# Leftover expert blocks: the down projection of one block stands behind the up projection of the next

## The chip, the cores and the metric

The kernel runs on one core of one Trainium2 chip. TensorE (PE) multiplies matrices, VectorE (DVE) and ScalarE (ACT) work on tiles, GpSimd (POOL) issues the transfers whose rows are picked by an index (gathers and scatters), SyncE (SP) issues most of the plain ones. Each engine carries out its own instructions in the order in which the program lists them, and they meet through semaphores. The metric is the device time of one execution in microseconds.

## The reference

One layer of a decoder on 512 tokens of width 1024: a mixer (three causal branches, gated, projected back and added to the stream) and then a mixture of experts. Only the second half touches the change:

```
h     = adaLN-modulated rmsnorm(x)                       # 512 x 1024
ids, weight = the top 8 of 64 experts for each token     # group-limited, sigmoid
for expert e, for each token t that chose it:
    y = ((silu(h[t] @ w1[e]) * (h[t] @ w3[e])) @ w2[e])  # 1024 -> 256 -> 1024
    out[t] += 2.5 * weight * y
out += shared expert(h)
result = rmsnorm(x + gate * out, final_norm)
```

## The kernel before, in words

The mixer fills the first part of the span. Then a router sorts the tokens by expert, and its result lies in a table in memory: for each run of up to 128 tokens of one expert, the tokens' numbers and their weights, which are loaded on chip as `idxw`. The runs are worked off in two stages. The stage of pairs takes most of them (`pair_of_runs`). What is left, runs that found no place in a pair, is the **leftover stage**: 96 blocks are written out, block i inside `tc.If(n_left > i)`, each If nested in the one before (L1369 to L1371), so that the program jumps out of the nest after the last block there is. With this input nine blocks run, 0 to 8. All of it stands under `tc.manual_schedule()`: what an engine carries out is in the order in which the code is written.

One block takes 128 rows of tokens through one expert, in fp32 by splitting a number into a high and a low part:

- `load_up` (SP): w1 and w3 of block i+2 into `ra[i % 2]`, two transfers of 1 MB each. `load_down` (SP, L1012): w2 into `rad`, 1 MB.
- **Up projection** (PE, L1153 to L1155): 24 matmuls of 128x512 (eight steps of k; high by high, high by low, low by high), out of `mT` (the block's rows, transposed and split; `h2T` in the code) and `wh`, `wl` (the split weights) into `ph`. The weights of block i+1 are split meanwhile (`split_a`: `wh` by ACT L49, `wl` by DVE L50).
- `act_a`: silu (ACT L1162), then the product with the other half and the token's weight (DVE L1163) into `hw`.
- `x_a` twice: eight transposes (PE L1146) of `xg`, the rows gathered for block i+1, and their split into `mT` (ACT L49, DVE L50).
- `turn_b`: two transposes of `hw` (PE L1278) and a copy to `hb` (ACT L1280).
- `gather_a` (POOL): a copy of the token numbers for block i+2 (L1118) and their gather into `xg` (L1120).
- `down_b`: four matmuls, `hb` by w2 (PE L1288, each fp32 matmul is two records in the trace), and the product with the layer's gate into `y` (DVE L1289, two halves).
- `add_a` (POOL L1191): the scatter that adds `y` to the rows of `acc2` in memory.

POOL's gathers and scatters go through one software queue (q0 in the profile), the plain loads through another (q1). Behind the nest `acc2` is read back (`rc<-acc`, L1378, SP and ACT), the sum is normed and written out.

Of the kernel before, what the change touches and what calls it, by code (L numbers as in the profile page):

```python
# [20 lines left out]
P = 128  # L21
# [13 lines left out]
def trunk(ctx, tc, x, c, ada_w, ada_b, norm1, norm2, w_in, conv_a_w, conv_a_b, ln_a_g, ln_a_b,  # L35
# [796 lines left out]
    def rt(shape, name, dt=F32, bufs=1, tag=None):  # L832
        return hp.tile([P] + shape, dt, name=name, bufs=2 if tag in ("x1", "h2", "tm", "hf2") else bufs, tag=tag or name)
# [198 lines left out]
    V.scalar_tensor_tensor(cls[:, 1], svf, 64.5, cls[:, 2], op0=OP.is_lt, op1=OP.mult)  # L1032
    for j in range(2):
        V.tensor_tensor_scan(cum[:, j], ones, cls[:, j], (2.0, 0.0)[j], op0=OP.mult, op1=OP.add)
    nn_, mi = rt([2], "nn_"), rt([3], "mi", I32)
    V.scalar_tensor_tensor(mi[:, 0:1], cum[:, 0, P - 1:], 31.0, cum[:, 1, P - 1:], op0=OP.min, op1=OP.min)
    V.tensor_scalar(mi[:, 1:2], mi[:, 0:1], 1, None, op0=OP.logical_shift_right)
    V.tensor_scalar(nn_[:, 0:1], mi[:, 1:2], 2.0, None, op0=OP.mult)
# [8 lines left out]
    V.tensor_tensor(L[:, 0], cls[:, 2], lf[:, 0], op=OP.subtract)  # L1047
    V.tensor_tensor_scan(cl_, ones[:, 0:1].to_broadcast([P, 2 * P]), L.rearrange("p a e -> p (a e)"), nn_[:, 1:2], op0=OP.mult, op1=OP.add)
    V.tensor_copy(mi[:, 2:3], cl_[:, 2 * P - 1:])
    it, jk2, th = rt([5], "it"), rt([2 * P], "jk2", tag="tm"), rt([1], "th")  # L1050
    V.scalar_tensor_tensor(jk2[:, :P], cum[:, 0], iop, ones, op0=OP.is_le, op1=OP.mult, accum_out=it[:, 0:1])
    V.scalar_tensor_tensor(jk2[:, :P], cum[:, 1], iop, ones, op0=OP.is_le, op1=OP.mult, accum_out=it[:, 1:2])
# [25 lines left out]
    for a, src in enumerate((v_, c_)):  # L1078
# [1 line left out]
        for j in range(3):  # L1080
            T.matmul(ips[:, j], src[:, j:j + 1], ident, start=True, stop=True)
        V.tensor_copy(iv[:, a], ips)
    V.tensor_copy(items[:, 6, 0:2], mi[0:1, 1:3])
    hst.close()
    rawst.close()


    n_four = nc.values_load(items[0:1, 6, 0:1], min_val=0, max_val=15)
    n_left = nc.values_load(items[0:1, 6, 1:2], min_val=0, max_val=NL)
    ep = est.enter_context(tc.tile_pool(name="ep", bufs=1))  # L1090
    psx = est.enter_context(tc.tile_pool(name="psx", bufs=1, space=PSUM))
    xg = [ep.tile([P, D], F32, name=f"xg{b}") for b in range(2)]
# [22 lines left out]
    def gather_a(row, j, n=2):  # L1115
        s = j % 2
        cl = G.value_load(items[0:1, row + 1, j:j + 1], min_val=0, max_val=4 * E - 1)
        G.tensor_copy(ia[s], idxw[:, ds(cl, 2)])  # L1118
        for b in range(n):
            G.indirect_dma_start(out=xg[b], out_offset=None, in_=h2d, in_offset=IOA(ap=ia[s][:, b, 0:1], axis=0),  # L1120
                                 bounds_check=S - 1, oob_is_err=False)

    def gather_c(row, j):
        s = j % 2
# [6 lines left out]
    def slots(src, shape, name):  # L1131
        t = ep.tile([P] + shape, I32, name=name, bufs=2)
        V.tensor_copy(t, src)
        return t

    def split_a(j, u, up=None):
        if u < 4:
            src = (up or ra[j % 2]).rearrange("p (z k f) -> p k z f", z=2, k=KT)[:, 2 * u:2 * u + 2]
            split(*(w[u].rearrange("p (k z f) -> p k z f", k=2, z=2) for w in (wh, wl)), src)
        else:  # L1140
            split(wh[u], wl[u], rad[j % 2][:, (u - 4) * 1024:(u - 3) * 1024])

    def x_a(b, g):
        pt = psx.tile([P, 4, P], F32, name="pt", bufs=2)
        for k in range(4):
            T.transpose(pt[:, k], xg[b][:, (g * 4 + k) * P:(g * 4 + k + 1) * P], ident)  # L1146
        split(h2T[0][b][:, g * 4:g * 4 + 4], h2T[1][b][:, g * 4:g * 4 + 4], pt)
# [42 lines left out]
    def add_a(y, at, beside=None, to=acc):  # L1190
        st = G.indirect_dma_start(out=to, out_offset=IOA(ap=at, axis=0), in_=y, in_offset=None,  # L1191
                                  compute_op=OP.add, bounds_check=S - 1, oob_is_err=False)
        g = beside or f"run {st.ins.name}"
        if beside:
            tc.declare_no_dep(st.ins, group=g, reason="the rows of a run are distinct")
        tc.add_to_no_dep_group(g, st.ins)
        return g
# [77 lines left out]
    def turn_b(hw):  # L1275
        p3 = pse.tile([P, 2, 2, P], F32, name="p3")
        for k in range(2):
            T.transpose(p3[:, 0, k], hw[:, k * P:(k + 1) * P], ident)  # L1278
        hb = ew.tile([P, 2, P], F32, name="hb", tag="hh")
        A.activation(hb, p3[:, 0], AF.Copy)  # L1280
        return hb

    def down_b(i, hb):
        y = ew.tile([P, D], F32, name="y", bufs=2)
        for h in range(2):
            py, q = pse.tile([P, 512], F32, name="py", bufs=2), slice(h * 512, h * 512 + 512)
            for k in range(2):
                T.matmul(py, hb[:, k], rad[i % 2][:, k * 1024 + h * 512:k * 1024 + h * 512 + 512], start=(k == 0), stop=(k == 1))  # L1288
            V.tensor_tensor(y[:, q], py, gm2[:, q], op=OP.mult)  # L1289
        return y  # L1290

    def block(i):
        if i:
            load_up(ra, GL, i + 2)
        up = rc[0] if i == 1 else None
        ph = ps_up((0,))
        for u in range(4):
            up_a(ph, u)
            if u < 3:
                split_a(i + 1, u, up)  # L1300
        hw = act_a(ph[0], ia[i % 2][:, 0, 1:2])
        sa = slots(ia[i % 2], [2, 2], "sa")
        split_a(i + 1, 3, up)
        x_a(0, 0)
        x_a(0, 1)
        hT = turn_b(hw)
        gather_a(GL, i + 2, 1)
        add_a(down_b(i, hT), sa[:, 0, 0:1], to=acc2)
        load_down(rad[i % 2], GL, i + 2)

    gs, tok = rad[1][:, :D], ew.tile([P, TT], I32, name="tok")
    nc.sync.dma_start(gs, modr[3:4].to_broadcast([P, D]))
# [25 lines left out]
    with tc.manual_schedule():  # L1338
        gather_a(GA, 0)
        copied = gather_c(GC, 0)  # L1340
        for t in range(2):
            run = add_a(ysh[t], tok[:, t:t + 1], run)
        load_up(rc, GC, 0, copied)
        load_down(rcd, GC, 0)
        for g in range(4):
            x_a(g // 2, g % 2)
        gather_a(GA, 1)
        nc.sync.dma_start(fn[0:1], final_norm[None, :])
        A.activation(gm2, gs, AF.Copy)
        for z in range(2):  # L1350
            zq = slice(z * CH, z * CH + CH)
            A.activation(gm2c[zq], gs[zq, z * 512:z * 512 + 512], AF.Copy)
        for t in range(2, TT):
            run = add_a(ysh[t], tok[:, t:t + 1], run)
        for u in range(6):
            split_a(0, u)
        load_down(rad[1], GA, 1)
        with ExitStack() as nest:
            for i in range(15):
                nest.enter_context(tc.If(n_four > i))  # L1360
                pair_of_runs(2 * i)
                pair_of_runs(2 * i + 1)

        nc.scalar.dma_start(rc[1].rearrange("p (t d) -> p t d", t=TT), acc.rearrange("(t p) d -> p t d", p=P))
        for h in range(2):
            py, q = pse.tile([P, 512], F32, name="py", bufs=2), slice(h * 512, h * 512 + 512)
            T.matmul(py, ones[0:1], fn[0:1, q], start=True, stop=True)
            A.activation(fn[:, q], py, AF.Copy)
        with ExitStack() as nest:  # L1369
            for i in range(NL):  # L1370
                nest.enter_context(tc.If(n_left > i))  # L1371
                block(i)


    fs = ew.tile([P, TT], F32, name="fs")
# [41 lines left out]
```

## Time and profile before

| what | us |
| --- | --- |
| median of three runs | 1458.77 (1456.04 to 1461.76) |
| the profiled execution, its time | 1467.86 |
| the profiled execution, its span | 1466.1 |
| leftover stage, first up matmul of block 0 to the read of `acc2` | 1328.65 to 1445.83 |
| one block of it | 11.84 |

The prediction is worked out inside the profiled execution and then set against the median. Starts in the rows below count from the start of its span.

### The profile page before, as it was taken

To read this page: it belongs to the slowest core of one execution; us is meant where nothing else is said; L and a number is where in the kernel's file an instruction comes from. 1 tells how busy PE (TensorE), PEld (TensorE's weight loads), DVE (VectorE), ACT (ScalarE), POOL (GpSimd) and SP (SyncE) were. 2 spreads that over 40 slices of the span, in tenths; PEclk is the share of its full clock that TensorE was granted. 3 is DMA by queue.
4 is the path that set the end of the run, shared out by engine and by line. 5 is a ranking of instruction groups with operands and counts; after the bars stand their busy time and mean duration, and the time that the engine had idled before them with its cause. 6 is when DMAs were issued, how large, how long until landed. Compare 5 with 4: busy or idle time off the path is not lost. (4 is left out here: it accounts for less than half of the span.)

```text
span 1466.1 us, 24089 instructions
## 1 busy us (share of the span) xinstructions
PE 1347.5 (92%) x8982; PEld 968.7 (66%) x8982; DVE 956.0 (65%) x1816; ACT 620.3 (42%) x1019; POOL 264.8 (18%) x255
## 2 busy tenths in 40 slices
PE   4999999999999979998998978999999999997881
PEld 3877777776766756664686635777677777774660
DVE  6865998987777777233455855666656566564664
ACT  4454334427568658220212213434434443443442
POOL 1000000000000000000000354243342524333332
PEclk8999999999999989999999989999999999999996
DMA  9321231232112117759826348999898989966985
GB/s 339 110 58 31 66 89 47 69 125 92 31 59 80 31 51 237 242 185 333 278 74 238 134 154 266 371 341 322 322 313 294 314 301 337 321 219 206 317 285 208
DMA packets 120634, 289.13 MB, mean 197 GB/s; under 512 B 14883, under 2 KB 68397, under 8 KB 109486
## 3 DMA queue, kind: packets, MB, share of 16 engines
q1 hardware_dynamic: 99266, 242.87, 46.2%
q0 software_dynamic: 17904, 36.01, 10.0%
q10 hardware_dynamic: 3324, 8.49, 1.6%
q8 instruction: 75, 1.23, 0.3%
q14 instruction: 65, 0.53, 0.1%
HBM read 260.24 MB, written 46.97 MB: 210 GB/s over the span
## 5 line engine op out<-in xcount | busy, mean ns | idle before, releaser
L53 PE MATMUL ps_in<-hT_hi,w_hi 128*128 128x512 f32 x496 | 203.9, 411 | 2.7 <-ACT hT_hi L49 2.7
L54 PE MATMUL ps_in<-hT_hi,w_lo 128*128 128x512 f32 x496 | 201.5, 406 | 0.3 <-DVE w_lo L50 0.2
L55 PE MATMUL ps_in<-hT_lo,w_hi 128*128 128x512 f32 x496 | 199.9, 406 | 0.0
L50 DVE TENSOR_TENSOR wl<-ra,wh 128x1024 fp32r<-128x1024 f32 x100 | 122.1, 1224 | 115.2 <-ACT wh L49 111.6
L49 ACT ACTIVATE wh<-ra 128x1024 fp32r<-128x1024 f32 x100 | 105.6, 1060 | 127.8 <-PE ph L1155 90.0
L1153 PE MATMUL ph<-wh,mT_hi 128*128 128x512 f32 x328 | 134.5, 410 | 2.3 <-ACT wh L49 2.3
L1154 PE MATMUL ph<-wl,mT_hi 128*128 128x512 f32 x328 | 129.6, 395 | 0.5 <-DVE wl L50 0.5
L1155 PE MATMUL ph<-wh,mT_lo 128*128 128x512 f32 x328 | 129.3, 394 | 0.0
L50 DVE TENSOR_TENSOR w_lo<-w_raw,w_hi 128x1024 fp32r<-128x1024 f32 x76 | 92.5, 1223 | 51.0 <-ACT w_hi L49 50.8
L53 PEld LDWEIGHTS ps_in<-hT_hi,w_hi 128*128 128x128 f32 x496 | 94.6, 191 | 34.3 <-issue 7.6
L1191 POOL DMA_INDIRECT acc<-y,sa x41 | 65.6, 1599 | 272.9 <-DVE hc L1227 238.0
L54 PEld LDWEIGHTS ps_in<-hT_hi,w_lo 128*128 128x128 f32 x496 | 94.4, 190 | 21.7 <-issue 1.7
L55 PEld LDWEIGHTS ps_in<-hT_lo,w_hi 128*128 128x128 f32 x496 | 94.3, 190 | 21.8 <-issue 2.7
L49 ACT ACTIVATE w_hi<-w_raw 128x1024 fp32r<-128x1024 f32 x76 | 79.3, 1052 | 38.8 <-PE ps_p L55 18.3
L594 DVE SCALAR_TENSOR_TENSOR u<-ut,par,u 128x512 f32<-128x512 f32 x120 | 84.2, 747 | 0.6
L70 POOL TENSOR_TENSOR h<-h,mhalf 128x4 f32<-128x4 f32 x8 | 10.5, 1310 | 358.4 <-DVE h L393 358.4
L1153 PEld LDWEIGHTS ph<-wh,mT_hi 128*128 128x128 f32 x328 | 62.7, 191 | 18.2 <-issue 3.4
L1154 PEld LDWEIGHTS ph<-wl,mT_hi 128*128 128x128 f32 x328 | 62.8, 191 | 15.3 <-issue 1.9
L1155 PEld LDWEIGHTS ph<-wh,mT_lo 128*128 128x128 f32 x328 | 62.6, 191 | 13.3
L1187 DVE TENSOR_TENSOR y<-py,rows 128x512 f32<-128x512 f32 x64 | 44.1, 689 | 31.9 <-PE py L1185 25.1
L49 ACT ACTIVATE wh<-rad 128x1024 fp32r<-128x1024 f32 x34 | 34.1, 1050 | 71.8 <-issue 36.1
L1120 POOL DMA_INDIRECT xg<-h2d,ia x45 | 56.3, 1250 | 20.3 <-issue 8.8
(523 smaller groups left out, 2754.5 us busy)
## 6 DMA issues: line engine op xcount, KB each, us to landing
ra<-in_exp_w_dram SPq DMA_DIRECT2D x52, 1024.0 KB
rc<-in_exp_w_dram SPq DMA_DIRECT2D x34, 1024.0 KB
w_raw<-in_w_in_dram SPq DMA_DIRECT2D x31, 1024.0 KB
rad<-in_exp_w_dram SPq DMA_DIRECT2D x27, 1024.0 KB
adar<-in_ada_w_dram SPq DMA_DIRECT2D x32, 512.0 KB
rcd<-in_exp_w_dram SPq DMA_DIRECT2D x16, 1024.0 KB
ada<-in_ada_w_dram SPq DMA_DIRECT2D x8, 1024.0 KB
gd<-sg SPq DMA_DIRECT2D x24, 256.0 KB
```

The source lines that it names most:

```text
L49: A.activation(hi, src, AF.Copy)
L50: (lo_engine or V).tensor_tensor(lo, src, hi.bitcast(F32), op=OP.subtract)
L53: T.matmul(ps, l[0], r[0], start=first, stop=False)
L54: T.matmul(ps, l[1], r[0], start=False, stop=False)
L55: T.matmul(ps, l[0], r[1], start=False, stop=last)
L594: V.scalar_tensor_tensor(u[:, ct], ut[ct][:, w:w + S], col("caw", w * 4 + ct), u[:, ct], op0=OP.mult, op1=OP.add)
L1120: G.indirect_dma_start(out=xg[b], out_offset=None, in_=h2d, in_offset=IOA(ap=ia[s][:, b, 0:1], axis=0), bounds_check=S - 1, oob_is_err=False)
L1153: T.matmul(ph[b], h2T[0][b][:, k], wh[u][:, q], start=(k == 0), stop=False)
L1154: T.matmul(ph[b], h2T[0][b][:, k], wl[u][:, q], start=False, stop=False)
L1155: T.matmul(ph[b], h2T[1][b][:, k], wh[u][:, q], start=False, stop=(k == KT - 1))
L1187: V.tensor_tensor(y[:, q], py, gate[:, q], op=OP.mult)
L1191: st = G.indirect_dma_start(out=to, out_offset=IOA(ap=at, axis=0), in_=y, in_offset=None, compute_op=OP.add, bounds_check=S - 1, oob_is_er ...
```

## The change

In a leftover block the down projection is no longer the block's own. Block i now does, in this order: up projection, `act_a`, a copy of its slots to `sb[i % 2]`, the last weight split, the copy of the token numbers for the gather, then `down_b(i-1)`, `add_a` of its result and `load_down` for block i+1; then `turn_b` of its own `hw` into `hbk` (a buffer that lasts from block to block and lies on `xc`, which the stage doesn't use), `x_a`, and last the gather. Block 0 has no down projection ahead of it. The last block's down projection follows behind the nest, in one of two branches: `last_even` and `last_odd` (each 0 or 1, from the number of leftovers) choose which of the two `rad` and `sb` it reads. Three small DVE instructions work those two numbers out, and two more values are read from `items`.

```
@@ routing: the two numbers
+    V.tensor_scalar(mi[:, 5:6], mi[:, 2:3], 1, None, op0=OP.logical_shift_right)
+    V.scalar_tensor_tensor(mi[:, 3:4], mi[:, 5:6], -2.0, cl_[:, 2 * P - 1:], op0=OP.mult, op1=OP.add)
+    V.scalar_tensor_tensor(mi[:, 4:5], cl_[:, 2 * P - 1:], 0.5, mi[:, 3:4], op0=OP.is_gt, op1=OP.subtract)
...
+    last_even, last_odd = (nc.values_load(items[0:1, 6, i:i + 1], min_val=0, max_val=1) for i in (2, 3))
@@ the gather in two parts: the numbers now, the transfer when it is called
+    def gather_rows(row, j):
+        s = j % 2
+        cl = G.value_load(items[0:1, row + 1, j:j + 1], min_val=0, max_val=4 * E - 1)
+        G.tensor_copy(ia[s], idxw[:, ds(cl, 2)])
+        return lambda: G.indirect_dma_start(out=xg[0], out_offset=None, in_=h2d, in_offset=IOA(ap=ia[s][:, 0, 0:1], axis=0),
+                                            bounds_check=S - 1, oob_is_err=False)
@@ turn_b, down_b
-        hb = ew.tile([P, 2, P], F32, name="hb", tag="hh")
-        A.activation(hb, p3[:, 0], AF.Copy)
-        return hb
+        A.activation(hbk, p3[:, 0], AF.Copy)
-    def down_b(i, hb):
+    def down_b(i):
-                T.matmul(py, hb[:, k], rad[i % 2][...], start=(k == 0), stop=(k == 1))
+                T.matmul(py, hbk[:, k], rad[i % 2][...], start=(k == 0), stop=(k == 1))
@@ block
         hw = act_a(ph[0], ia[i % 2][:, 0, 1:2])
-        sa = slots(ia[i % 2], [2, 2], "sa")
+        V.tensor_copy(sb[i % 2], ia[i % 2])
         split_a(i + 1, 3, up)
+        gather = gather_rows(GL, i + 2)
+        if i:
+            add_a(down_b(i - 1), sb[(i - 1) % 2][:, 0, 0:1], to=acc2)
+            load_down(rad[(i - 1) % 2], GL, i + 1)
+        turn_b(hw)
         x_a(0, 0)
         x_a(0, 1)
-        hT = turn_b(hw)
-        gather_a(GL, i + 2, 1)
-        add_a(down_b(i, hT), sa[:, 0, 0:1], to=acc2)
-        load_down(rad[i % 2], GL, i + 2)
+        gather()
@@ behind the nest
+        for z, last in enumerate((last_even, last_odd)):
+            with tc.If(last > 0):
+                add_a(down_b(z), sb[z][:, 0, 0:1], to=acc2)
```

On PE, in an inner block, from the end of its up projection to the start of the next one. Before:

```order
L1155 MATMUL ph<-wh_8068,mT_lo_5784 128x512
L1146 MATMUL pt<-ident,xg_7935 128x128 x8
L1278 MATMUL p_16346<-ident,hw 128x128 x2
L1288 MATMUL py<-rad_7752,hb 128x512 x4
L1369 COMPARE_AND_BRANCH
L1153 MATMUL ph<-wh_8065,mT_hi_5782 128x512
```

The same place now (`xc` is where `hbk` lies):

```order
L1167 MATMUL ph<-wh_8101,mT_lo_5784 128x512
L1298 MATMUL py<-rad_7753,xc 128x512 x4
L1290 MATMUL p_16370<-ident,hw 128x128 x2
L1158 MATMUL pt<-ident,xg_7966 128x128 x8
L1384 COMPARE_AND_BRANCH
L1165 MATMUL ph<-wh_8098,mT_hi_5782 128x512
```

The four down matmuls moved from the end of the stretch to its head, with the other `rad`; the eight transposes of the next block's rows, which stood first, are now the last thing ahead of the next up projection.

On POOL, in an inner block, from one branch of the nest on, with what each instruction waits for. Before:

```order
L1369 COMPARE_AND_BRANCH
L1117 TENSOR_LOAD items
L1117 ISA x2
L1118 ISA
L1118 COPY ia_7953<-idxw 128x4 [waits DVE_49]
L1120 DMA xg_7935<-h2d,ia_7953 128x1024 [waits DMASW3_49,DMASW5_49,PE_49,Pool_49]
L1191 DMA acc_73<-y,sa 512x1024 [waits DMASW6_49,DMASW4_49,DVE_49]
```

And now:

```order
L1384 COMPARE_AND_BRANCH
L1130 TENSOR_LOAD items
L1130 ISA x2
L1131 ISA
L1131 COPY ia_7984<-idxw 128x4 [waits DVE_49]
L1203 DMA acc_73<-y,sb_7989 512x1024 [waits DMASW2_49,DVE_49]
L1132 DMA xg_7966<-h2d,ia_7984 128x1024 [waits DMASW3_49,DMASW5_49,PE_49,Pool_49]
```

The gather (`xg<-h2d`) stood ahead of the block's scatter (`acc<-y`); now the scatter of the block before stands ahead of the gather.

On PE, the end of the stage. Before, the last down projection and the jumps out of the nest:

```order
L1288 MATMUL py<-rad_7753,hb 128x512 [waits DMAHW3_49,Activation_49]
L1288 MATMUL py<-rad_7753,hb 128x512 x3
L1369 UNCONDITIONAL_BRANCH
L1369 UNCONDITIONAL_BRANCH [waits PE_49] x96
L1413 UNCONDITIONAL_BRANCH
```

And now, up to the end of the first branch behind the nest:

```order
L1158 MATMUL pt<-ident,xg_7966 128x128 x3
L1384 UNCONDITIONAL_BRANCH
L1384 UNCONDITIONAL_BRANCH [waits PE_49] x96
L1094 TENSOR_LOAD items
L1389 COMPARE_AND_BRANCH
L1298 MATMUL py<-rad_7752,xc 128x512 [waits DMAHW2_49,DMAHW3_49,DMAHW0_49,DMAHW4_49,DMASW7_49,DMAHW5_49,DMASW3_49,DMAHW6_49,DMASW2_49,DMAHW7_49,DVE_49,Activation_49]
L1298 MATMUL py<-rad_7752,xc 128x512
L1298 MATMUL py<-rad_7752,xc 128x512 [waits DVE_49]
L1298 MATMUL py<-rad_7752,xc 128x512
L1389 UNCONDITIONAL_BRANCH
```

The four matmuls stood ahead of the jumps; now they stand behind them, behind the reading of a value and a branch, and wait for DVE, ACT and the counters of the plain and the software transfers (`DMAHW`, `DMASW`).

## Rows read from the trace of the kernel before

**Rows 1.** The page: the span, and the busy share of PE in 40 equal slices of it, in tenths. One slice is 36.7 us; the leftover stage lies in the 37th to the 39th and a part of the 40th.

```profile
span 1466.1 us, 24089 instructions
PE   4999999999999979998998978999999999997881
```

**Rows 2.** Busy time by stretch, for three of the eight full blocks: start and end, length, then for PE, PEld, DVE, ACT and POOL the busy time and (number) of instructions, then the granted clock, the DMA engines' share and GB/s.

```profile
1341.75:1353.59 11.84, 10.48 (x44) 7.08 (x43) 7.85 (x10) 5.76 (x8) 3.78 (x3) 1.00 0.89 297
1377.27:1389.11 11.84, 10.48 (x44) 7.08 (x43) 7.67 (x10) 5.65 (x8) 3.77 (x3) 1.00 0.96 327
1424.72:1436.60 11.88, 10.52 (x44) 7.06 (x42) 7.85 (x10) 5.77 (x8) 3.77 (x3) 1.00 0.76 286
```

**Rows 3.** The timeline of PE in order of time, from the end of block 0's up projection on: start, length, engine, line, operation, out<-in, count, and in brackets the idle time ahead of it with what ended it. The first two rows are block 0, the next three block 1, then the first matmul of block 2 and the transposes of block 8. A matmul is listed until its result is out, so rows overlap by some 0.2 us.

```profile
1335.79 1.03 PE L1146 MATMUL pt<-ident,xg 128*128 128x128 f32 x8
1337.44 0.44 PE L1278 MATMUL p<-ident,hw 128*128 128x128 f32 x2 [0.62 <-DVE hw L1163]
...
1341.75 0.80 PE L1153 MATMUL ph<-wh,mT_hi 128*128 128x512 f32 x1
...
1347.62 1.03 PE L1146 MATMUL pt<-ident,xg 128*128 128x128 f32 x8
...
1350.45 3.70 PE L1288 MATMUL py<-rad,hb 128*128 128x512 f32 x8 [0.74 <-ACT hb L1280]
1353.59 0.80 PE L1153 MATMUL ph<-wh,mT_hi 128*128 128x512 f32 x1
...
1430.63 1.03 PE L1146 MATMUL pt<-ident,xg 128*128 128x128 f32 x8
```

**Rows 4.** The timelines of ACT (two rows) and DVE (two rows) in block 1: the split of the next rows into high and low (each x2), the copy of `hb`, the second half of `y`. Ahead of them one small step of DVE in the routing.

```profile
876.33 0.16 DVE L1070 SCALAR_TENSOR_TENSOR v__7874<-b__7876,v__7874 128x3 f32<-128x3 f32 x1
...
1349.05 1.08 ACT L49 ACTIVATE mT_hi<-pt 128x512 fp32r<-128x512 f32 x2
1350.01 0.40 ACT L1280 ACTIVATE hb<-p 128x256 f32<-128x256 f32 x1
1350.34 1.28 DVE L50 TENSOR_TENSOR mT_lo<-pt,mT_hi 128x512 fp32r<-128x512 f32 x2
1354.19 0.69 DVE L1289 TENSOR_TENSOR y<-py,rows 128x512 f32<-128x512 f32 x1 [1.02 <-PE py L1288]
```

**Rows 5.** The timeline of POOL: the scatter of block 0, the gather issued in block 1, the scatter of block 1, the scatter of block 8.

```profile
1343.32 1.59 POOL L1191 DMA_INDIRECT acc<-y,sa  x1 [3.34 <-DVE y L1289]
...
1350.74 1.08 POOL L1120 DMA_INDIRECT xg<-h2d,ia  x1 [0.27 <-POOL ia L1118]
...
1355.16 1.58 POOL L1191 DMA_INDIRECT acc<-y,sa  x1 [3.34 <-DVE y L1289]
...
1438.17 1.59 POOL L1191 DMA_INDIRECT acc<-y,sa  x1 [3.34 <-DVE y L1289]
```

**Rows 6.** What the DMA queues moved (packets, MB, share of the 16 engines' time) in three stretches after the scatter of block 0: 1343.0 to 1348.3 (the first row is all there is; no q0 row), then 1348.3 to 1353.4 (the next two), then 1353.4 to 1356.6 (the last two).

```profile
q1 hardware_dynamic: 323, 1.47, 82.7%
...
q1 hardware_dynamic: 188, 1.38, 68.7%
q0 software_dynamic: 139, 0.33, 34.4%
...
q1 hardware_dynamic: 103, 0.52, 50.9%
q0 software_dynamic: 149, 0.40, 32.0%
```

**Rows 7.** The stage of pairs, where two gathers are issued straight behind a scatter: POOL's timeline, then the queues from 1187.4 to 1192.5 (q1 alone, no q0 row) and q0 from 1192.5 to 1196.7.

```profile
1187.35 1.59 POOL L1191 DMA_INDIRECT acc<-y,sa  x1 [14.50 <-DVE hc L1227]
...
1189.42 1.08 POOL L1120 DMA_INDIRECT xg<-h2d,ia  x1 [0.28 <-POOL ia L1118]
...
q1 hardware_dynamic: 267, 1.93, 98.8%
...
q0 software_dynamic: 219, 0.83, 82.2%
```

**Rows 8.** SP's own queue (SPq) of issues: `load_down` of block 8, and the read of `acc2`.

```profile
1437.19 0.38 SPq L1012 DMA_DIRECT2D rad<-in_exp_w_dram  x1
...
1445.83 0.84 SPq L1378 DMA_DIRECT2D rc<-acc  x2
```

**Rows 9.** The instructions of L1369, the nest's own line, from 1432 to 1447: engine, operation, count: shortest/median/longest in ns, start of the first and of the last. They are the jumps out of the nest and the operations on counters that stand there.

```profile
L1369 SPq EVENT_SEMAPHORE  x9: 17/17/17, 1443.4 to 1444.0; - x9
...
L1369 PEldq COMPARE_BRANCH  x2: 193/1998/3804, 1433.5 to 1437.5; - x2
...
L1369 SPq COMPARE_BRANCH  x2: 43/46/50, 1437.6 to 1444.1; - x2
...
L1369 POOLq INC_SWDGE_SEM  x1: 1446/1446/1446, 1443.9 to 1443.9; - x1
```

**Rows 10.** PE at the start of the leftover stage, behind an idle stretch: busy time of the stretch (columns as in rows 2), then from the timelines the first four matmul records there and two single weight loads of them, one record apart.

```profile
1325.05:1331.90 6.85, 6.85 (x12) 3.62 (x13) 0.00 (x0) 1.27 (x3) 0.00 (x0) 0.51 0.28 38
...
1325.05 3.67 PE L1367 MATMUL py<-rows,ones 1*128 1x512 f32 x4 [5.05 <-DVEq L1358]
...
1325.96 0.33 PEld L1367 LDWEIGHTS py<-rows,ones 1*128 1x128 f32 x1 [0.52 <-issue]
1326.82 0.33 PEld L1367 LDWEIGHTS py<-rows,ones 1*128 1x128 f32 x1 [0.53 <-issue]
```

More of the change, by code (lines that the diff above doesn't have):

```diff
@@ L1034, in trunk @@
         V.tensor_tensor_scan(cum[:, j], ones, cls[:, j], (2.0, 0.0)[j], op0=OP.mult, op1=OP.add)
-    nn_, mi = rt([2], "nn_"), rt([3], "mi", I32)
+    nn_, mi = rt([2], "nn_"), rt([6], "mi", I32)
     V.scalar_tensor_tensor(mi[:, 0:1], cum[:, 0, P - 1:], 31.0, cum[:, 1, P - 1:], op0=OP.min, op1=OP.min)
@@ L1082, in trunk @@
         V.tensor_copy(iv[:, a], ips)
-    V.tensor_copy(items[:, 6, 0:2], mi[0:1, 1:3])
+    V.tensor_copy(items[:, 6, 0:4], mi[0:1, 1:5])
     hst.close()
@@ L1287, in down_b @@
             for k in range(2):
-                T.matmul(py, hb[:, k], rad[i % 2][:, k * 1024 + h * 512:k * 1024 + h * 512 + 512], start=(k == 0), stop=(k == 1))
+                T.matmul(py, hbk[:, k], rad[i % 2][:, k * 1024 + h * 512:k * 1024 + h * 512 + 512], start=(k == 0), stop=(k == 1))
             V.tensor_tensor(y[:, q], py, gm2[:, q], op=OP.mult)
@@ L1301, in block @@
         hw = act_a(ph[0], ia[i % 2][:, 0, 1:2])
-        sa = slots(ia[i % 2], [2, 2], "sa")
+        V.tensor_copy(sb[i % 2], ia[i % 2])
         split_a(i + 1, 3, up)
+        gather = gather_rows(GL, i + 2)
[3 more added lines that the diff above has]
+        turn_b(hw)
         x_a(0, 0)
         x_a(0, 1)
-        hT = turn_b(hw)
-        gather_a(GL, i + 2, 1)
-        add_a(down_b(i, hT), sa[:, 0, 0:1], to=acc2)
-        load_down(rad[i % 2], GL, i + 2)
+        gather()
+    hbk, sb = xc.rearrange("p (a k s) -> p a k s", a=2, k=2)[:, 0], [ep.tile([P, 2, 2], I32, name=f"sb{i}") for i in range(2)]
     gs, tok = rad[1][:, :D], ew.tile([P, TT], I32, name="tok")
```

## The prediction

> **What bounds the kernel now.** I first read the page: PE is busy in nearly all slices of the span [rows 1], so in the leftover stage, too, the question is what PE waits for. The busy time by stretch says that: a block lasts 11.84 us and PE is busy for 10.5 of them, at a granted clock of 1.00, while DVE has 7.9, ACT 5.8, POOL 3.8 [rows 2]. The DMA engines are at 0.76 to 0.96 of their time: a second bound, not far off. PE's timeline shows where its 1.4 us go [rows 3]: 0.62 us ahead of the transposes of `hw` (DVE's product is late) and 0.74 us ahead of the down projection (ACT's copy `hb` is late). The other gaps are under 0.1 us. I call U the end of a block's up projection, where its transposes start before: U0 = 1335.79, U1 = 1347.62, U8 = 1430.63. The tail counts from there too: `acc2` is read at 1445.83 [rows 8], U8 + 15.2.
>
> **Block 0** loses its down projection. Its transposes of `hw` stay at 1337.44, and those of the next rows follow at 1337.7, over 1.0 us [rows 3]. A half of the split costs ACT 0.54 and DVE 0.64 [rows 4], so with some 0.1 us per hand-over the next up projection can start 1.35 us behind the first transpose, and its third matmul, which reads the low half, 2.05 behind. An up projection is 24 matmuls in 5.87 us, the first with a head start of 0.4 [rows 3]: 0.228 each. U1 = 1337.7 + 2.05 + 22 x 0.228 = 1344.8, **2.8 us earlier**.
>
> **An inner block, if nothing holds it.** Behind U stand the eight records of the down projection (3.70 less the overlap of 0.25, so 3.45 [rows 3]), two transposes (0.27), then the next rows' transposes at X = U + 3.7, and the next U at X + 2.05 + 5.0 = X + 7.05. The period is 10.76. Both waits are gone, since the down projection's operand is a block old and covers the product of `hw`; a wait of some 0.3 us for the first split rows takes a part back.
>
> **What holds it.** `x_a` now stands directly ahead of the up projection that needs it, and POOL issues the scatter of block i-1 ahead of the gather. `y` is done 0.69 [rows 4] behind the down projection's last record, at U + 4.35, so the scatter is issued at U + 4.6 and the gather, which waits for the transposes of `xg` in any case, behind it at about U + 6.5 (POOL spends 1.6 on a scatter [rows 5]). How long the scatter then keeps q0 busy, block 0 shows: issued at 1343.32 [rows 5], no packet of it in 5 us, while q1 moves 1.47 MB; then 139 packets up to 1353.4; and the gather that was issued at 1350.74 mostly behind that [rows 6]. That is 10.1 us from the scatter's issue, so the gather's rows land at U + c, with c from 15 to 17.9. The low end is the stage of pairs, where after 5.1 us without a packet q0 moves 0.83 MB in 4.2 us [rows 7]: a scatter and a gather of 0.5 MB each, at that rate, need about 5.1, so 4.6 + 10.2 = 14.8 or some 15. The high end adds the whole 3.2 us of the last stretch to 14.7 [rows 6]. I take 16.0, since half of the 0.5 MB of a gather is moved in half that stretch and the rest lies beside the scatter's end. These rows are needed in the next block at X, that is at U + 10.76 + 3.7 = U + 14.5. So the rows are late, and two chains, each two blocks long, set the pace: U(i+2) = U(i) + c + 7.05. The period is (16.0 + 7.05) / 2 = 11.5 (11.0 to 12.5 at the ends). With seven periods U8 = 1344.8 + 80.5 = 1425.3, **5.3 us earlier** than before (1422.0 to 1432.3).
>
> Here a rule speaks against the row. The Trainium skill ("DMA: Bandwidth & Descriptors", section "Queues, rings and completion order") says that each DMA engine goes round its queue rows packet by packet. By that rule a scatter would start beside `load_up`'s packets and the gather's rows would land in time, with a period of 10.76; the trace does not agree where it shows no q0 packet in 5 us.
>
> **The tail.** Before, the last down projection stood ahead of the jump out of the nest. Now the jump stands between. The nest's own line shows its price [rows 9]: PE's branch took 3.80 us, and SP went from its branch at 1437.6 to its first counter at 1443.4, 5.8 us, with nine operations on counters up to 1444.0 and a branch behind. The matmuls behind the nest wait for SP's counters too, as their list of waits shows. SP issues its last load at about U8 + 3.7 now (when the down projection of block 7 has read `rad`), so it is through at 3.7 + 0.4 + 5.8 + 0.7 = U8 + 10.6, and PE, whose last transposes end at U8 + 4.7, stands idle for 5.5 us or more. What a cold start costs stands at the stage's head: behind 5.05 us idle the clock was 0.51 for 6.85 us, the lower of its two levels, and records came 0.86 us apart [rows 10]. Eight of them plus the drain: 8 x 0.86 + 0.2 = 7.1, so U8 + 17.7; the second half of `y` 0.73, U8 + 18.5; POOL's issue at + 0.28; the scatter lands. Its landing comes from the end before: issued at 1438.17 [rows 5], behind it POOL's operation on its own counter at 1443.9 [rows 9], so 5.7. With 0.4 for SP's wake and issue, `acc2` is read at U8 + 24.85 in place of U8 + 15.2, **9.65 us later**. Low end: at full clock 8 x 0.43 in place of 8 x 0.86, 3.4 less, and if PE need not wait for SP but only for its own jump (4.7 + 3.8 = U8 + 8.5, less a little), 2 to 2.7 less. High end: 1.8 more, if POOL's jump and its counter operation of 1.45 [rows 9] stand on the path for the second branch.
>
> **Small things.** Three DVE instructions of a few elements stand in the routing chain, which PE waits on: a step of their like takes 0.16 [rows 4], so 0.3 us as they overlap, not over 0.5. The copy to `sb` replaces the one to `sa`. Holds of 1 to 2 us in the blocks may cost clock: 0.5. The order of `load_up`, scatter and `load_down` within a period stays, so I cost the loads at nothing; what covers it is the DMA share's remainder, 0.04 to 0.24 of a period [rows 2], and if it is used up the period stays near 11.84.
>
> **The sum**: -5.3 + 9.65 + 0.3 + 0.5 = +5.2 on the profiled execution's 1467.86. That execution was 9 us above the median of the three timed ones, and I set the difference against the median: 1458.77 + 5.2 = **1464**. What a measurement of this kernel can tell from no change is about 0.5%, 7.3 us, so the bounds are 1451.5 and 1466.1.
>
> **The rivals.**
> - *The rows are not held* (0.20): q0's packets get their turn beside q1's, or the scatter is through sooner than in block 0. The period is 10.76, U8 = 1344.8 + 75.3 = 1420.1, 10.5 earlier; with the tail's 9.65 and 0.3 it comes out at 1458. For it: q0 moves 0.33 MB beside q1's 1.38 once it has started [rows 6]. Against: both places with no q0 packet in 5 us [rows 6, 7].
> - *The rows are held longer* (0.25), slower: at c = 16.6 the period is 11.83, as before, and from there on the blocks give nothing beyond block 0. At c = 17.9 U8 is 1432.3, 1.7 later; plus 9.65, 0.3 and 0.5 that is 12 us, 1470. For it: the DMA engines are nearly full, and a period that asks the same bytes in less time finds less room. Against: the last blocks have 0.76 [rows 2].
> - *The tail is cheap* (0.13): the last down projection starts with PE's own jump or earlier and at the full clock, and `acc2` is read near U8 + 16. Then the sum is -5.3 + 0.7 + 0.8, 1455. For it: the branch instructions themselves take 0.04 us [rows 9]. Against: PE's of 3.80 in the same row, and rows 10. The Trainium skill ("Advanced Engine Details and Errata", section "Control Flow Timing") gives about 108 ns for a compare-and-branch; by that the jump would be hidden and the time would be this rival's, but PE's row of 3804 ns does not agree.
> - *As forecast* (0.42), by its own bounds 1460 to 1469.
>
> **How the numbers follow.** The forecast is the likeliest case, 1464. The range from 1456 to 1471 takes in the case without a hold (1458) and most of the longer hold, and leaves out the cheap tail and mishaps on top. Faster needs under 1451.5: a cheap tail with no hold, 0.07. Slower, above 1466.1: most of the longer hold and the upper third of the forecast, 0.35. The rest, 0.58, is within 0.5%.
>
> **What would show it.** Right: PE waits ahead of L1158 for `xg`, 0.5 to 1.5 us in most blocks, and no longer ahead of L1290 and L1298; U1 near 2.8 us earlier; a period of 11.0 to 11.9; behind the nest an idle PE of 5 us or more, then eight records at 0.86 apart at a clock near 0.5; `acc2` read some 24 us behind U8. Wrong: q0's packets of the scatter beside `load_up`'s; a period of 10.8; or a last down projection within 6 us of the last transposes at the full clock. If the stage before it or the mixer move by over 1 us, a cause that I have not seen is at work.

## The result and the profile after

The changed kernel is slower: a median of 1473.39 us (1471.46 to 1475.82) beside 1457.4 for the kernel before, a ratio of **1.0096 with a 95% interval of 1.0073 to 1.012**, 14 us. That lies outside my range (1456 to 1471), beyond the slow rival.

The page of the changed kernel, with the span and the busy share of PE in 40 slices:

```profile
span 1471.1 us, 24118 instructions
...
PE   4999999999999979998998988999999999988881
```

The span is only 5 us longer than the one of before [rows 1], since the profiled execution of before had 9 us more ahead of the leftover stage (its first matmul there starts at 1325.05, now at 1316.10). So I compare the stage by itself, from that matmul to the read of `acc2`: 120.78 us before, 134.63 now, **13.85 more**, which agrees with the 14 of the ratio. Parts of the stage differ by some 3 us between executions (the section on the experiments has a pair), so an agreement to a tenth is luck.

The timeline of PE now, from block 1 to block 4, and the transposes in block 7 (columns as in rows 3; all matmuls of the up projections but the first left out):

```profile
1335.90 3.60 PE L1298 MATMUL py<-rad,xc 128*128 128x512 f32 x8
1339.33 0.38 PE L1290 MATMUL p<-ident,hw 128*128 128x128 f32 x2
1339.55 1.04 PE L1158 MATMUL pt<-ident,xg 128*128 128x128 f32 x8
1340.89 0.50 PE L1165 MATMUL ph<-wh,mT_hi 128*128 128x512 f32 x1 [0.30 <-ACT mT_hi L49]
...
1346.74 3.60 PE L1298 MATMUL py<-rad,xc 128*128 128x512 f32 x8
...
1353.93 1.94 PE L1158 MATMUL pt<-ident,xg 128*128 128x128 f32 x8 [3.38 <-DMA xg<-h2d,ia]
...
1361.89 3.60 PE L1298 MATMUL py<-rad,xc 128*128 128x512 f32 x8
...
1379.84 1.06 PE L1158 MATMUL pt<-ident,xg 128*128 128x128 f32 x8 [3.25 <-DMA xg<-h2d,ia]
...
1417.19 1.06 PE L1158 MATMUL pt<-ident,xg 128*128 128x128 f32 x8 [2.39 <-DMA xg<-h2d,ia]
```

U, the start of the down projection, is 1335.90 in block 1, 1346.74 in block 2, 1361.89 in block 3: one block of 10.84, as worked out for the unhindered case, then one of 15.15. The waits for `hw` and `hb` [rows 3] are gone, and in their place PE stands for the gathered rows: 3.38 us in block 2, 3.25 in block 4, 0.88 in block 6 and 2.39 in block 7. The busy time by stretch shows what the idle time brings with it (columns as in rows 2): block 1 and block 2, block 7, a part of block 7 behind its wait, and the last down projection.

```profile
1335.90:1346.74 10.84, 10.54 (x44) 7.02 (x43) 7.85 (x11) 5.99 (x8) 3.77 (x3) 1.00 0.67 234
1346.74:1361.89 15.15, 11.77 (x44) 8.21 (x42) 7.95 (x11) 6.09 (x8) 3.77 (x3) 0.89 0.96 339
...
1410.98:1427.63 16.65, 13.70 (x44) 8.98 (x42) 7.79 (x11) 6.05 (x8) 3.77 (x3) 0.79 0.77 256
1418.55:1425.30 6.75, 6.48 (x14) 4.63 (x15) 3.25 (x5) 2.04 (x3) 2.67 (x2) 0.50 0.94 329
1439.70:1446.37 6.67, 6.67 (x8) 2.49 (x8) 0.69 (x1) 0.00 (x0) 0.00 (x0) 0.55 0.01 2
```

The granted clock, 1.00 in all blocks of before [rows 2], is 0.89 in blocks 2 and 4, 0.79 in block 7, and 1.00 in block 6 with its short wait. Behind the longer waits PE works for a time at the lower of its two levels (0.50 for 6.75 us in block 7), and its busy time for the same 44 records is 1.2 to 3.2 us longer.

POOL and DVE in blocks 1 and 2, from their timelines (POOL's rows first):

```profile
1340.50 1.60 POOL L1203 DMA_INDIRECT acc<-y,sb  x1 [1.76 <-DVE y L1299]
1342.41 1.07 POOL L1132 DMA_INDIRECT xg<-h2d,ia  x1 [0.30 <-issue]
1351.59 1.11 POOL L1131 COPY ia<-idxw 128x4 int32 x1 [8.10 <-DVE sb L1313]
1354.12 1.59 POOL L1203 DMA_INDIRECT acc<-y,sb  x1 [1.43 <-DVE y L1299]
...
1347.86 0.47 DVE L1175 SCALAR_TENSOR_TENSOR hw<-hw,ia,ph 128x256 f32<-128x256 f32 x1
1351.35 0.17 DVE L1313 COPY sb<-ia 128x4 int32<-128x4 int32 x1 [3.02 <-DMA acc<-y,sb]
1351.43 1.22 DVE L50 TENSOR_TENSOR wl<-ra,wh 128x1024 fp32r<-128x1024 f32 x1
1352.56 1.28 DVE L1299 TENSOR_TENSOR y<-py,rows 128x512 f32<-128x512 f32 x2
```

In block 1 the scatter goes out 4.6 us behind U and the gather 6.5, to the tenth as worked out. In block 2 there is a wait that my prediction does not have at all: **DVE stands 3.02 us at the copy of the slots**. `sb` has two buffers, the one for block 2 is still read by block 0's scatter, issued at 1340.50 (the same wait is 4.39 us in block 4 and 4.31 in block 7), and behind the copy on DVE stand a weight split and the product `y`; so block 1's scatter, which needs `y`, goes out at U + 7.4, and the gather behind it later still. Before, `sa` had two buffers as well, but the scatter went out a block earlier and had landed.

The queues from 1340.5 to 1345.0 (one row: no q0), from 1345.0 to 1353.5 (two rows), and from 1353.5 to 1359.0 (q1 alone again), as in rows 6:

```profile
q1 hardware_dynamic: 318, 1.43, 90.1%
...
q1 hardware_dynamic: 318, 2.03, 64.3%
q0 software_dynamic: 288, 0.73, 33.3%
...
q1 hardware_dynamic: 379, 2.12, 101.0%
```

Again nothing of the scatter passes for 4.5 us, and scatter and gather then take 8.5 us side by side with the loads. The two move 0.73 MB and not 1.0, so their runs are not full ones of 128 tokens. Not all of the 4.5 us comes from the loads: the scatter of block 8 is issued at 1447.38, when no queue moves anything, and has no packet before 1449.5 either. It is a small one, as its queue row from 1449.5 to 1450.4 shows (packets, MB, share):

```profile
q0 software_dynamic: 144, 0.01, 11.6%
```

The tail, from PE's, SP's and POOL's timelines and, for the last row, from the chain that ended last:

```profile
1439.70 6.67 PE L1298 MATMUL py<-rad,xc 128*128 128x512 f32 x8 [7.38 <-SPq L1384]
...
1431.26 0.38 SPq L1012 DMA_DIRECT2D rad<-in_exp_w_dram  x1
1450.73 0.82 SPq L1396 DMA_DIRECT2D rc<-acc  x2
...
1447.38 1.57 POOL L1203 DMA_INDIRECT acc<-y,sb  x1 [12.18 <-DVEq L1389]
...
1447.38 3.00 DMA acc<-y,sb
```

With U8 = 1427.63 PE starts the last down projection at U8 + 12.1, cold, eight records in 6.67 us; `acc2` is read at U8 + 23.1 against 15.2 before [rows 8]. So of the 13.85 us the tail has 7.9 and the blocks have 5.95 (U8 is 111.53 behind the stage's first matmul, before 105.58).

### The profile page after: what moved, and what is told of

The parts are those of the page before. It is cut to its first block, busy times and chain, and to the rows that moved or that the text cites. A ratio compares the mean times of both kernels' runs of the same rounds, so it can differ in the third digit from the quotient of the medians.

```text
span 1471.1 us, 24118 instructions
## 1 busy us (share of the span) xinstructions
PE 1353.8 (92%) x8982; PEld 972.0 (66%) x8982; DVE 954.9 (65%) x1819; ACT 622.1 (42%) x1019; POOL 264.2 (18%) x255
## 5 line engine op out<-in xcount | busy, mean ns | idle before, releaser
L1203 POOL DMA_INDIRECT acc<-y,sa x32 | 51.2, 1600 | 242.7 <-DVE hc L1239 237.8
L50 DVE TENSOR_TENSOR mT_lo<-pt,mT_hi 128x512 fp32r<-128x512 f32 x86 | 55.5, 686 | 7.9 <-ACT mT_hi L49 7.4
```

The lines of the kernel that those rows point to most:

```text
L50: (lo_engine or V).tensor_tensor(lo, src, hi.bitcast(F32), op=OP.subtract)
```

## The experiments

All kernels are variants of the changed one. The ratio is to the kernel before on the same chip in the same hours, which matters here: the kernel before itself had medians from 1457 to 1469. The stage and its parts are from one profiled execution each; two kernels with the same code in their blocks (the changed one and the run without the tail) differ by 3 us in U1 to U8, so parts of that size are read with care. In kernels that have the transposes first, U is their start.

| kernel | stage | U1 to U8 | U8 to the read | ratio, 95% interval |
| --- | --- | --- | --- | --- |
| before | 120.78 | 83.0 | 15.2 | 1 |
| changed | 134.63 | 91.7 | 23.1 | 1.0096 (1.0073 to 1.012) |
| e1, four slots | 131.51 | 88.7 | 21.9 | 1.0085 (1.0058 to 1.0113) |
| e2, two row buffers | 135.59 | 94.8 | 21.1 | 1.0084 (1.0059 to 1.0109) |
| e3, both | 120.18 | 76.1 | 23.4 | 0.9973 (0.9951 to 0.9995) |
| e4, transposes first | 124.56 | 78.0 | 24.3 | 1.0013 (0.9991 to 1.0034) |
| e5, gather first | 122.95 | 78.5 | 23.9 | 0.9983 (0.9961 to 1.0005) |
| e6, no tail | 123.45 | 88.8 | 13.5 | 1.0008 (0.9989 to 1.0028) |
| e7, gather at the head | 118.12 | 74.4 | 24.5 | 0.9971 (0.9948 to 0.9994) |
| e8, tail in the nest | 122.26 | 83.1 | 19.4 | 1.0014 (0.9993 to 1.0035) |
| e9, warm tail | 118.35 | 76.2 | 22.3 | 0.9973 (0.995 to 0.9996) |
| e10, e7 and the tail in the nest | 114.48 | 75.7 | 19.5 | 0.9955 (0.9937 to 0.9972) |

**e1, four copies of the slots.**

```
-  V.tensor_copy(sb[i % 2], ia[i % 2])
+  V.tensor_copy(sb[i % 4], ia[i % 2])      # and sb[(i - 1) % 4] for the scatter, four buffers
```

> The changed kernel with four copies of the slots (sb) in place of two, so that DVE's copy no longer waits for the scatter of two blocks before; with the nine leftover blocks of this input the last block still finds its slots. In the changed kernel DVE stands up to 3.0 us ahead of that copy, and the scatter behind it goes out at U + 4.6 to U + 8.8. Theory A (two causes: the gather's rows pass behind the scatter, and the slots' wait makes the scatter itself late): every scatter goes out at U + 4.6 to 5, the rows land at U + 16.5 on average in place of 18, the period falls from 13.1 to about 12.4, and the time by 4 to 6 us, to about 1468. Rival B (the order in the queue alone; the rows would be as late without the slots' wait): under 1.5 us, 1472 to 1474.

**e2, two buffers for the gathered rows, the gather ahead of the scatter.**

```
-  gather = gather_rows(GL, i + 2)
+  gather_rows(GL, i + 2)()                 # into xg[(i + 1) % 2]; no gather() at the end
-  x_a(0, 0); x_a(0, 1); gather()
+  x_a(0, 0, xg[i % 2]); x_a(0, 1, xg[i % 2])
```

> The changed kernel with two buffers for the gathered rows, used in turn, so that the gather is issued ahead of the scatter, at about U + 3; sb stays at two. Theory A: no wait of PE for the gathered rows is left, but DVE still stands 2 to 4 us at the copy of the slots, and the next rows' low half is split behind that; period 11.5 to 12.5, time 1463 to 1469. Rival B (the order in the queue alone): the period is 10.8 to 11, and the time 1457 to 1459. Rival C (the loads' bytes are the bound, whatever the order): the period stays at 12.5 or more and PE or the splits wait for weights; 1470 to 1474.

**e3, both.**

> Both: two row buffers with the gather ahead of the scatter, and four copies of the slots. Theory A and rival B: the unhindered period of 10.8, so 2.3 x 7 = 16 us less than the changed kernel, 1457 to 1459 with the tail as it is; e1 and e2 each give a part of it by A, e2 alone all of it by B. Rival C: 1468 or more, and the waits move to the weights.

Neither edit alone gives anything that the ratios can tell: 1.0085 and 1.0084, beside 1.0096. Both together give all, a ratio of 0.9973 and blocks of 10.84, with six of seven periods within 0.01 of it. So theory A's sizes were wrong (it gave each edit a part), and so is e2's rival B, by which e2 alone would have done. In e1 its own rival B is nearer: the scatter goes out at U + 4.6 in blocks 1, 3 and 6, and the rows are still there only 17.97, 17.66 and 17.57 us behind U, where theory A has 16.5. The wait for the slots is not what makes the rows late. What each run is left with stands in its rows. In e1 PE still waits for the gathered rows; in e2 it does not, but DVE stands at the copy of the slots and PE gets the low half of the next rows too late; in e3 only the 0.3 us for the first split is left. PE of e1, then DVE and PE of e2, then PE of e3:

```profile
1363.24 1.06 PE L1158 MATMUL pt<-ident,xg 128*128 128x128 f32 x8 [3.30 <-DMA xg<-h2d,ia]
```

```profile
1372.57 0.17 DVE L1314 COPY sb<-ia 128x4 int32<-128x4 int32 x1 [3.35 <-DMA acc<-y,sb]
...
1375.71 0.79 PE L1168 MATMUL ph<-wh,mT_lo 128*128 128x512 f32 x1 [2.37 <-DVE mT_lo L50]
```

```profile
1372.45 0.50 PE L1166 MATMUL ph<-wh,mT_hi 128*128 128x512 f32 x1 [0.30 <-ACT mT_hi L49]
...
1383.29 0.50 PE L1166 MATMUL ph<-wh,mT_hi 128*128 128x512 f32 x1 [0.30 <-ACT mT_hi L49]
```

These are two holds side by side, each long enough by itself to keep the blocks at 12.7 to 13.5 us, and both hang on the scatter: one through the queue that the gather shares with it, the other through the buffer that it reads its indices from. Rival C falls too: the same bytes pass in blocks of 10.84.

**e4, the transposes first, as in the kernel before, and four slots.** `x_a` and the gather stand ahead of `down_b(i-1)`.

> The transposes of the next rows stay where the kernel before has them, first behind the up projection, and the gather goes out ahead of the scatter from one row buffer; only the down projection is moved (a block later), with four copies of the slots. PE then has no split to wait for ahead of the up projection. Theory A: a period of 10.2 to 10.8, time 1452 to 1458 with the tail's 8 us. Rival C (bytes): 11.5 or more, 1462 or more.

Ratio 1.0013, with periods from 10.0 to 14.7. Blocks without a wait have the forecast 10.0, but in four blocks PE stands for the rows, which it now needs 4 us sooner, twice for 0.3 and 0.9 us, and twice for longer:

```profile
1348.57 1.06 PE L1158 MATMUL pt<-ident,xg 128*128 128x128 f32 x8 [2.86 <-DMA xg<-h2d,ia]
...
1383.33 1.14 PE L1158 MATMUL pt<-ident,xg 128*128 128x128 f32 x8 [3.58 <-DMA xg<-h2d,ia]
```

The ratio lies between the two cases that I had written down, and the theory's 1452 to 1458 was too good.

**e5, one row buffer, the gather ahead of the scatter, four slots.** Only the order on POOL differs from e1.

```
-  add_a(down_b(i - 1), ...); load_down(...); turn_b(hw); x_a(0, 0); x_a(0, 1); gather()
+  y = down_b(i - 1); load_down(...); turn_b(hw); x_a(0, 0); x_a(0, 1); gather(); add_a(y, ...)
```

> One row buffer, the order on PE as in the changed kernel, four copies of the slots; only on POOL the gather, which can go out when the transposes have read the buffer (about U + 5.3), stands ahead of the scatter (about U + 6.5). It tells what helped in the run with two row buffers and four copies (10.84 a block): the place ahead of the scatter, or the issue 3 us earlier from a buffer of its own. Theory Q (the place in the queue): the gather's rows land by about U + 13, no wait at the transposes, a period of 10.8 to 11.1 and a ratio to the kernel before of 0.997 to 1.000. Rival E (the early issue; behind SP's loads a gather at U + 5.3 is late too): rows at U + 16 or later, a period of 12 or more, ratio 1.006 or more.

Ratio 0.9983 against 1.0085 of e1: most of the gain comes from the place ahead of the scatter, although the gather goes out only 5.4 to 6.6 us behind U. That is theory Q, with a mean period of 11.2, just above its 11.1. What is missing to e3's 76.1 shows on PE, which waits 0.3 to 0.96 us for the rows, and on POOL, where two gathers stand until the scatter before them has landed (3.75 and 2.59 us):

```profile
1350.19 1.06 PE L1158 MATMUL pt<-ident,xg 128*128 128x128 f32 x8 [0.96 <-DMA xg<-h2d,ia]
...
1352.01 1.06 POOL L1132 DMA_INDIRECT xg<-h2d,ia  x1 [3.75 <-DMA acc<-y,sb]
```

**e6, without the tail.**

> The changed kernel without the two branches behind the nest, so the last block's down projection and its scatter are left out (its rows miss one expert's part). It measures the tail by itself. If the tail's cost is the jump plus the cold down projection plus the scatter, acc2 is read 13 to 15 us behind the last up projection in place of 23.1, and the time falls by 8 to 10 us, to a ratio of about 1.003 to the kernel before. If most of it is the jump, which stays, it is read at 18 or later and the time falls by 5 or less.

`acc2` is read 13.5 us behind the last up projection, so the tail costs 9.6 us (23.1 less 13.5), within what was expected if jump, cold matmuls and scatter stand in a row; the ratio falls by 0.0088, or 12.8 us with an uncertainty of some 4. Even so this kernel, which does less work, is no faster than before: the blocks' holds have eaten what the moved down projection gave. The read, with U8 at 1425.08:

```profile
1438.55 0.82 SPq L1393 DMA_DIRECT2D rc<-acc  x2
```

**e7, the transposes first, the gather at the head of the block.** Two row buffers, four copies of the numbers `ia`, four slots.

> The transposes of the next rows first behind the up projection, as in the kernel before, and the gather at the head of the block, ahead of its up projection, into two row buffers by four copies of the numbers; four copies of the slots; the down projection a block late and the tail as in the changed kernel. Theory: nothing but PE's own work is left in a block, a period of 10.0 (the shortest of the run with the transposes first, which waited for its rows in three blocks), so 0.84 x 8 = 6 us less than the run at 10.84, ratio 0.992 to 0.994. Rival (the loads' bytes bound the stage below 10.8): a period of 10.5 or more, waits at the weights, ratio 0.996 or more.

The stage is 118.12, ratio 0.9971. Three periods are 10.0, but the others are 10.6 to 11.75; PE waited once for the rows (0.95 us) and else mostly 0.3 to 0.9 for the low half of the next rows, which DVE split only behind a weight split. Rival and theory each have a part: the bytes do not bound it at 10.8, but 10.0 is not held.

**e8 and e10, the last down projection inside the nest.**

```
+  with tc.If(n_left < i + 2):              # at the end of every block
+      add_a(down_b(i), sb[i % 4][:, 0, 0:1], to=acc2)      # e10: down_b(i, rcd[:, :D])
-  for z, last in enumerate((last_even, last_odd)): ...
```

> Two row buffers and four copies of the slots, as in the run at 10.84 a block, but the last down projection stands inside the nest, at the end of every block, in a branch that is taken in the last block alone; the two branches behind the nest are gone. If the jump out of the nest is what makes the tail dear, acc2 is read at 15 to 17 us behind the last up projection in place of 23, 6 to 8 us less; what speaks against is a branch more in every block, on each engine, with its counters: at 0.3 us a block 3 us come back, at 1.5 us (POOL's counter operation) all of the gain goes. Expected: ratio 0.993, or 0.999 and above if the branch costs a block 1 us.

> The run with the transposes first and the gather at the head of the block (four copies of numbers and slots), and the last down projection at the end of each block in a branch that only the last block takes, with a result buffer of its own (rcd, which this stage does not use), where the earlier run with such a branch shared the two buffers of y and DVE waited up to 2.4 us for a scatter. Theory: the branch itself costs a block under 0.2 us, the last down projection starts within 6 us of the last up projection at the full clock, and acc2 is read at 18 to 19.5 in place of 24.4 behind the last up projection; stage 113 to 114 us in place of 118.1, ratio 0.993 to 0.995. Rival (the branch's cost in every block): a period longer by 0.5 or more, stage 117 or more, ratio 0.997 or more.

In e8 the last down projection starts 5.8 us behind U8 at the full clock, and `acc2` is read at 19.4, not 15 to 17; but the blocks lose 7 us against e3, since the product `y` in the branch takes one of two buffers and DVE then waits in six blocks for the scatter of the block before (0.63 to 2.67 us). The row of DVE in a block, and PE's of the last down projection:

```profile
1364.83 1.29 DVE L1300 TENSOR_TENSOR y<-py,rows 128x512 f32<-128x512 f32 x2 [2.42 <-DMA acc<-y,sb]
...
1426.31 3.67 PE L1299 MATMUL py<-rad,xc 128*128 128x512 f32 x8 [1.10 <-ACT mT_hi L49]
```

In e10 the branch has a buffer of its own. The shortest blocks are 0.6 us longer than in e7 (10.59 in place of 10.0), more than the 0.2 that I expected, and U1 to U8 is 1.3 longer. PE stands 0.31 us at the branch (L1324), the first row below. In e8 the branch costs nothing in the two blocks without a longer wait of PE (10.82 and 10.84, against 10.84 in e3): there PE stands 0.3 us for the first split at that place in any case. So what the branch costs hangs on what else PE waits for there. The tail's start is early as well:

```profile
1342.61 0.49 PE L1166 MATMUL ph<-wh,mT_hi 128*128 128x512 f32 x1 [0.31 <-PEq L1324]
...
1418.53 3.70 PE L1300 MATMUL py<-rad,xc 128*128 128x512 f32 x8 [0.53 <-ACT xc L1292]
...
1432.81 0.82 SPq L1396 DMA_DIRECT2D rc<-acc  x2
```

The stage takes 114.48 us and the kernel **0.9955 of the time before (0.9937 to 0.9972)**, 6 to 7 us less: this version beats both kernels.

**e9, a warm tail.** 18 small matmuls with an unread result in the branch behind the nest of e3, where PE stands idle (and one ahead of the nest, into the same tile).

> Two row buffers and four copies of the slots (the run at 10.84 a block), and in the branch behind the nest 18 small matmuls (128x128, their result unread) ahead of the last down projection, at the place where PE stood waiting for SP's counters from about 8.8 to 12.8 us behind the last up projection. They measure the clock's part of the tail. Theory: the eight records of the last down projection, 0.86 apart after the idle stretch (6.10 us in all), go faster by up to 3 us because PE is no longer cold, and acc2 is read at 20.5 to 22 in place of 23.4. Rival: the matmuls run at the lower clock themselves, 0.22 each, 4 us, and the clock rises no sooner: the down projection again takes 6 us and acc2 is read at 23 to 24.5. Ratio to the kernel before 0.995 to 0.998 either way.

```profile
1428.55 5.90 PE L1393 MATMUL phc<-ident 128*128 128x128 f32 x36 [3.91 <-PEq L1386]
1434.29 3.60 PE L1299 MATMUL py<-rad,xc 128*128 128x512 f32 x8
...
1428.55:1434.20 5.65, 5.65 (x36) 5.65 (x37) 0.00 (x0) 0.00 (x0) 0.20 (x1) 0.70 0.10 21
1434.29:1437.90 3.61, 3.60 (x10) 1.33 (x8) 0.69 (x1) 0.00 (x0) 0.00 (x0) 1.00 0.01 5
```

(The last two rows are the busy time by stretch.) The last down projection takes 3.60 us at a granted clock of 1.00, in place of 6.10 in e3: the cold clock costs 2.5 us there. The small matmuls themselves had a clock of 0.70, took 5.65 us and held the start up, so 1.1 us remain: `acc2` is read at 22.3. Each of the two cases had a part of it.

## Why the prediction was wrong

Two steps failed, both in the blocks: the hold of the gathered rows (9.9 us of waits in place of 5.2), and the clock in the blocks (5.9 us in place of 0.5). The tail came out 1.75 us cheaper than forecast. One by one:

- **Block 0**: 2.8 us earlier was forecast; U1 is 19.80 behind the stage's first matmul, before 22.57, so 2.77. Right.
- **The unhindered block**: 10.76 was worked out, 10.84 measured, in this kernel in blocks 1 and 5 (10.88 in block 3) and in e3 in nearly all. Right, and the waits of [rows 3] are gone.
- **The hold of the gathered rows**: the mechanism was right (two chains, each two blocks long; the rows behind the scatter), the term was mis-sized, and it failed at the step "I take 16.0". The rows are there 18.0, 18.0, 15.5 and 18.1 us behind U of the block that gathers them, in the four cases where PE waits for them, so three times just past the high end of my own bounds (17.9). PE waits 3.38, 3.25, 0.88 and 2.39, 9.9 us in all, where a period of 11.5 has 5.2. What was mis-sized is the moving. In block 1 the issue (U + 4.6) and the time without a packet (4.5 us, forecast 5.0) hold, but scatter and gather then need 8.5 us beside 2.03 MB of loads, and 7.4 in block 3 (1372.1 to 1379.5, beside 1.62 MB), where the forecast has 6.4 (5.1 up to U + 14.7, and 1.3 of the last stretch). I had scaled that by bytes, at 0.5 MB for each of the two. The bytes do not set it: q0 moved 0.73 MB for the two in block 1 and 0.21 in block 6 (1410.5 to 1416.5), and the rows came 18 us behind U both times. In block 6 the scatter itself went out 1.7 us late, by the wait for the slots; e1 has the rows as late without that wait.
- **The copy to `sb` "replaces the one to `sa`"**: this was wrong, as a step costed at nothing without asking when its buffer comes free. The scatter that reads it went out at U + 7.5 of its own block ([rows 5], 1355.16) and goes out at U + 15.4 now, 4.6 behind the next U, so it is still under way when its buffer is wanted for the block after that (DVE's 3.02 us). In the changed kernel PE's own four waits are all for the rows; e2 shows that this wait alone keeps the loss.
- **The clock in the blocks**: priced at 0.5, measured at about 5.9: U1 to U8 is 91.7 = 7 x 10.84 + 9.9 of waits + 5.9, and nearly all of those are in the blocks with a granted clock of 0.89 and 0.79: 0.9 in block 2, 1.4 in block 4, 3.4 in block 7 (16.65 = 10.84 + 2.39 + 3.4). This is the term that was off by the most; rows 10 had shown what an idle stretch does, and I applied it to the tail alone.
- **The tail**: 9.65 forecast, 7.9 measured. PE's start came at U8 + 12.1 (forecast 10.6; SP went from its branch at 1431.7 to its first counter at 1438.7, 7.0 in place of 5.8), the cold matmuls took 6.67 (7.1), and the scatter landed in 3.0 (5.7). My 5.7 was read from POOL's operation on its counter and not from a landing. The scatter of block 8 is small in both kernels (144 packets, 0.01 MB). Before, it was issued beside loads (0.80 MB of q1 from 1438.0 to 1441.0, no q0 packet), now with empty queues.
- **The rivals**: what came is "the rows are held longer", which I gave 0.25, at its far end (12 us), and 2 us beyond by the clock. The case without a hold did not come; that of the cheap tail neither. By "DMA: Bandwidth & Descriptors" of the Trainium skill, section "Queues, rings and completion order", an engine goes packet by packet round the queue rows that it has work for, so the scatter would have had its turns. The trace again shows no q0 packet in 4.5 us beside q1 at 90.1%; but some 2.1 of these pass with empty queues too, so it speaks against the rule only if the scatter's packets were ready behind that, which no run here shows.

With the terms as measured (-5.3, and the clock's 0.5, become +5.95; 9.65 becomes 7.9) the sum is the stage's 13.85, as it must be, since both are parts of it. Whether the 0.3 us in the routing came, or anything of a few us in another stage, cannot be told: the stage starts anywhere from 1313.19 to 1326.29 us in the runs, and the ratio's 14 us has an uncertainty of some 3.4. So the last sign of the prediction, a move of over 1 us ahead of the stage, could not be read from these runs.

That the clock's 5.9 us would go with the waits is shown by e3, where both are gone at once; how much the clock would cost at the same waits was not tried by itself. Nor was it settled why the scatter's packets start so late beside the loads, nor why a wait of 2.39 us cost more clock than one of 3.38.

## What to carry to other kernels

When a step is put off by one block, ask of every buffer that it reads, index tiles too, when that comes free now: here DVE gets the index buffer of a scatter back only when the scatter has landed, and two copies that were enough for a step in its own block may not be for one a block later. Where two transfers share a queue, issue the one that is needed first ahead of the other; here the order on POOL alone (e5 against e1) was worth 1% of the whole kernel. And work moved behind the exit of a long nest pays for the exit and for a cold TensorE: inside the nest, in a branch with its own buffers, the tail was 5 us shorter, and the stage 3.6, since the blocks pay for the branch (e10 against e7).

## What the runs showed of the hardware that was not expected

- A transfer through the software queue had its first packet some 2 us behind its issue with empty queues (block 8's scatter, 1447.38 to 1449.5; before, a gather of 0.46 MB issued at 1338.91, no packet of any queue up to 1340.6), and not yet 4.5 us behind it beside 1.43 MB of loads (the scatter issued at 1340.50). The small scatter of block 8 then landed 3.00 us behind its issue.
- How long PE waits does not alone tell what clock follows. The blocks with waits of 3.38, 3.25 and 2.39 us had a granted clock of 0.89, 0.89 and 0.79, and the shortest of the three lost most. In e8 a block with a wait of 1.55 us (and 0.31 shortly ahead of it) had 0.88, while in e2 one with a wait of 1.90 and in e5 one with 0.96 kept 1.00.
- A branch that is not taken, at the end of each block, made the shortest blocks 0.6 us longer in e10 (10.59 against 10.0) and no longer in e8 (10.82 against 10.84).
